# PEER layer on one core: the second product's loads asked for further ahead, and the routing replanned

## The chip, the cores and the metric

One Trainium2 chip, one core of it. The metric is the device time of one execution in microseconds (us), as the median of several runs. TensorE (PE) does matmuls; VectorE (DVE) and ScalarE (ACT) do elementwise work; GpSimd (Pool) and SyncE (SP) issue DMA transfers, each from a queue that it takes in order.

## The reference

A two-layer first block, a second block with sparse attention, and at its end the part that the change is in, a product-key expert layer (PEER) over 512 tokens of width 1024:

```python
def peer(hn, w_q, subkeys, u, v):
    H, K = PEER_HEADS, PEER_TOPK                      # 8, 16
    xt = hn.reshape(T, D)                             # 512 x 1024
    q = (xt @ w_q).reshape(T, H, 2, PEER_QDIM // 2)
    s = jnp.einsum('thcd,cnd->thcn', q, subkeys)      # 128 keys per half
    s1, i1 = lax.top_k(s[:, :, 0], K)
    s2, i2 = lax.top_k(s[:, :, 1], K)
    cand = (s1[..., :, None] + s2[..., None, :]).reshape(T, H, K * K)
    sc, ci = lax.top_k(cand, K)
    e1 = jnp.take_along_axis(i1, ci // K, axis=-1)
    e2 = jnp.take_along_axis(i2, ci % K, axis=-1)
    idx = e1 * PEER_NKEYS + e2                        # one of 16384 experts
    g = jax.nn.softmax(sc, axis=-1)
    ...
        a = jnp.einsum('cd,chkd->chk', xc, u[ic])
        act = jax.nn.gelu(a) * gc
        return jnp.einsum('chk,chkd->cd', act, v[ic])
```

All in float32.

## The kernel before

Activations are held transposed, features on partitions, tokens along the free axis. A float32 matmul is done as three with split operands (`mm3`): high weight with high and low activation, low weight with high activation. Weights come in units of 128x1024 (`wunit`): `raw` by a 512 KB load on SP's queue (three buffers), `wh` by a cast on ACT (line 279), `wl` by a subtraction on DVE (line 280). `lin2` is 24 matmuls over such a unit, at line 325.

`peer` computes 384 of the 512 tokens (SG) densely, over all 16384 experts, and the last 128 by gathers.

*Query loop* (line 1623): for each head a `lin2` with `wpq`, and the key scores go to `sco`.

*First product*: `up(e)`, e = 0 to 127 (line 1777): a `lin2` of 512 columns with unit `pu[e]`, GELU into tile `ga`; 384 of its columns are stored in DRAM as `GA[e]`, 128 in `GU[e]`. Beside it runs the routing, mostly on DVE: `route(b)` for each block of 128 tokens (the top 16 of each key half, 16 wide calls of `top16`; the candidates; the top 16 of them, 8 narrow calls; the expert numbers by compares; transposes to `e1T`, `e2T`, `gT`), and `weights(tb, share)` for 16 tokens at a time, which makes the dense gate matrix `G` in DRAM: one-hot tiles `ohA`, `ohB` (line 1736), `ohW`, a group of four matmuls for four tokens (line 1749; 96 groups in all), the two halves of the sum added into `gst` (lines 1752 and 1753), and one 1 MB write per 16 tokens on Pool's queue (line 1755, 24 of them). The routing is a generator that yields the DVE and ACT ns that a piece takes, and the loop at line 1788 puts an `up` into the program whenever the sum is above PEER_NS. Ups left when the routing is over follow in a row (line 1793). A scheduler then orders each engine's instructions; pools and their buffers set what waits for what.

*Second product*: 16 groups g of 8 experts-tiles. For each of the 8, the GELU values come back from `GA` (`gd`, 192 KB, line 1833), are multiplied in place by the group's gate block `gt` (1.5 MB of `G` in pieces of 512 B, line 1828), and split into a pair `hid` (lines 1854 and 1855; 18 buffers, so nine pairs). Then come 8 steps d, each a `lin2` of 384 columns with unit `pv[g, d]`. So there are 128 steps n = 8g + d.

*The last 128 tokens*: `rows(m)`, m = 0 to 31, gathers four tiles of 128 rows of v (`vr`, 512 KB each, eight buffers) with indirect loads on Pool; `acts(m)` gathers 4 x 128 single elements of `GU` into `ac` (four buffers) with indirect loads on Pool, then two multiplies on DVE make `az`; `sums(m)` is 16 matmuls at line 1823 that add into one accumulator. In before sums(m) stand behind step 4m + 2, and acts(m + 1) behind step 4m + 1.

## Time and profile before

| | us |
|---|---|
| median of 3 runs (3704.99 to 3709.06) | 3708.48 |
| the profiled execution | 3707.12 |
| its span | 3705.3 |
| PE busy in it | 3561.1 (96%) |
| DVE busy | 2351.8 (63%) |
| ACT busy | 1649.6 (45%) |
| Pool busy | 344.8 (9%) |
| query loop, from 2224.6 | 63.4 |
| first product with routing, 2288 to 3049 | 761 |
| no matmul, 3049 to 3071 | 22 |
| second product, 3071 to 3697 | 626 |

The stages are read off the timeline, from the first and the last instruction of a stage on PE. How to read such a profile: an engine that is busy all the time in a stage bounds it, whatever its share of the whole span; for an engine that isn't, each idle stretch has a releaser, the event that ended it, and following releasers back gives the chain of waits. A wait on the bounding engine is time lost, a wait on another engine need not be.

### The profile page before, as it was taken

What the parts mean: (1) busy time and instruction counts of PE and PEld (TensorE: products, weight loads), DVE (VectorE), ACT (ScalarE), POOL (GpSimd) and SP (SyncE); (2) the same over time, 40 slices, a digit from 0 to 9 for tenths busy, and PEclk for the clock granted to TensorE, in tenths of its full rate; (3) what the DMA queues carried; (4) which work ended last, traced back from release to release, by engine and by line L of the source; (5) the groups of instructions that cost most, each with busy time, mean ns of one, the idle gap of its engine ahead of it and who ended that gap; (6) DMA issues with size and microseconds to landing.
All of it is one profiled execution on the core that took longest, in us unless ns stands there. A gap on an engine that the chain in (4) does not pass through costs nothing.

```text
span 3705.3 us, 53755 instructions
## 1 busy us (share of the span) xinstructions
PE 3561.1 (96%) x20154; PEld 2972.7 (80%) x20154; DVE 2351.8 (63%) x4926; ACT 1649.6 (45%) x3172; POOL 344.8 (9%) x430
## 2 busy tenths in 40 slices
PE   8998999999999999998999999999999997999999
PEld 5866788888877788887878777778888876989898
DVE  5976644444688765556587568999676424555554
ACT  5267531121355742224456544568766422323332
POOL 0000000000000000000000100000000006444441
PEclk9999999999999999999999999999999998999999
DMA  6430332111242132223441242445554449888885
GB/s 213 129 114 12 117 111 74 63 63 63 86 140 90 48 129 93 95 97 121 122 131 61 75 137 84 142 161 174 188 182 167 172 152 305 302 296 295 301 301 180
DMA packets 245780, 536.03 MB, mean 145 GB/s; under 512 B 26656, under 2 KB 131424, under 8 KB 242320
## 3 DMA queue, kind: packets, MB, share of 16 engines
q1 hardware_dynamic: 215648, 426.66, 35.4%
q0 software_dynamic: 29872, 105.95, 7.6%
q8 instruction: 158, 2.59, 0.3%
q14 instruction: 102, 0.84, 0.1%
HBM read 461.09 MB, written 68.16 MB: 143 GB/s over the span
## 4 chain that ended last, share of the span: by engine, by line
PE 84%; DVE 8%; DMA 3%; ACT 3%; issue 1%; SPq 0%; POOL 0%; ACTq 0%; DVEq 0%
PE b L325 54%; PE a L325 19%; PE a L1823 2%; DVE wl L280 2%; PE b L470 1%; PE b L920 1%; DMA gd<-GA 1%; PE b L571 1%; PE a L1749 1%; PE b L909 1%; PE b L1368 1%; DMA mraw<-in_wmod_dram 1%; DVE gst L1753 1%; PE a L1128 0%; PE b L1177 0%
## 5 line engine op out<-in xcount | busy, mean ns | idle before, releaser
L279 ACT CAST wh<-raw 128x1024 fp32r<-128x1024 f32 (+2 forms) x531 | 546.9, 1031 | 1431.6 <-PE b L325 796.9
L280 DVE TENSOR_TENSOR wl<-raw,wh 128x1024 fp32r<-128x1024 f32 (+2 forms) x531 | 636.1, 1198 | 333.0 <-ACT wh L279 321.4
L325 PE MATMUL b<-hs,wh 128*128 128x512 f32 x2624 | 822.8, 395 | 4.4 <-ACT hs L1095 4.4
L325 PEld LDWEIGHTS b<-hs,wh 128*128 128x128 f32 x2624 | 489.2, 190 | 108.0 <-ACT hs L1095 5.3
L325 PE MATMUL b<-hid,wh 128*128 128x384 f32 x2048 | 534.1, 342 | 24.8 <-DMA gd<-GA 22.4
L325 PE MATMUL b<-hs,wl 128*128 128x512 f32 x1312 | 515.5, 393 | 0.0
L325 PEld LDWEIGHTS b<-hid,wh 128*128 128x128 f32 x2048 | 373.5, 189 | 53.5 <-ACT hid L1854 22.9
L325 PE MATMUL b<-hh,wh 128*128 128x256 f32 (+1 forms) x1160 | 366.1, 352 | 3.7 <-DVE V L843 2.2
L325 PE MATMUL a<-hh,wh 128*128 128x512 f32 (+1 forms) x1144 | 354.6, 348 | 9.5 <-DVE y L1049 7.2
L325 PE MATMUL b<-hl,wh 128*128 128x256 f32 (+1 forms) x1160 | 357.3, 345 | 0.3 <-DVE hl L537 0.3
L325 PE MATMUL b<-hid,wl 128*128 128x384 f32 x1024 | 348.7, 340 | 9.0 <-DVE wl L280 9.0
L325 PE MATMUL b<-hh,wl 128*128 128x256 f32 (+1 forms) x1160 | 356.0, 344 | 0.0
L325 PE MATMUL a<-hh,wl 128*128 128x512 f32 (+1 forms) x1144 | 349.6, 344 | 1.5 <-DVE wl L280 1.5
L325 PE MATMUL a<-hl,wh 128*128 128x512 f32 (+1 forms) x1144 | 350.3, 344 | 0.3 <-DVE hl L537 0.3
L325 PEld LDWEIGHTS b<-hs,wl 128*128 128x128 f32 x1312 | 248.4, 189 | 52.3 <-issue 0.2
L325 PEld LDWEIGHTS b<-hh,wh 128*128 128x128 f32 x1160 | 201.3, 189 | 44.2 <-issue 4.9
L325 PEld LDWEIGHTS a<-hh,wh 128*128 128x128 f32 x1144 | 197.0, 188 | 44.6 <-issue 13.9
L325 PEld LDWEIGHTS b<-hl,wh 128*128 128x128 f32 x1160 | 201.7, 189 | 30.4 <-issue 1.5
L325 PEld LDWEIGHTS b<-hh,wl 128*128 128x128 f32 x1160 | 201.1, 189 | 27.9 <-issue 1.1
L325 PEld LDWEIGHTS a<-hl,wh 128*128 128x128 f32 x1144 | 197.2, 188 | 31.0 <-issue 2.8
L325 PEld LDWEIGHTS a<-hh,wl 128*128 128x128 f32 x1144 | 196.9, 188 | 30.6 <-DVE wl L280 2.4
L325 PEld LDWEIGHTS b<-hid,wl 128*128 128x128 f32 x1024 | 193.8, 189 | 11.0 <-DVE wl L280 11.0
(427 smaller groups left out, 5332.6 us busy)
## 6 DMA issues: line engine op xcount, KB each, us to landing
raw<-in_w_dram SPq DMA_DIRECT2D x134, 512.0 KB
raw<-in_pu_dram SPq DMA_DIRECT2D x128, 512.0 KB
raw<-in_pv_dram SPq DMA_DIRECT2D x128, 512.0 KB
raw<-in_win_dram SPq DMA_DIRECT2D x64, 512.0 KB
mraw<-in_wmod_dram SPq DMA_DIRECT2D x82, 384.0 KB
GA<-ga SPq DMA_DIRECT2D x128, 192.0 KB
G<-gst POOLq DMA_DIRECT2D x24, 1024.0 KB, 4.7
gt<-G SPq DMA_DIRECT2D x16, 1536.0 KB
```

The source lines that it names most:

```text
L279: nc.scalar.copy(hi, raw)
L280: nc.vector.tensor_tensor(lo, raw, hi, op=OP.subtract)
L325: nc.tensor.matmul(o, w[wi], xx[xi], start=start and xi == 0 and wi == 0, stop=stop and wi == 1)
L470: nc.tensor.matmul(p[j:j + 32, 0:256], self.cs[:, k, :], ws[k], start=k < 4, stop=k >= 4, tile_position=(0, j))
L571: nc.tensor.matmul(p[:, :w], self.ones[1024], s, start=k == 0, stop=k == 7)
L909: nc.tensor.transpose(p[:, j * 128:j * 128 + 128], Ps[e][:, kc * 128:kc * 128 + 128], self.eye)
L920: nc.tensor.matmul(o[pr, c % 2 * 128:c % 2 * 128 + 128], V[i][:, kc, pr], PT[e * nkb + kc], start=kc == 0, stop=kc == nkb - 1, tile_positi ...
L1368: nc.tensor.transpose(p[:, j * 128:j * 128 + 128], src, self.eye)
L1749: nc.tensor.matmul(p[:, i * 256:i * 256 + 256], A[:, i], W[:, i].rearrange("p j e -> p (j e)"), start=True, stop=True)
L1753: nc.vector.tensor_tensor(gst[:, :, t8:t8 + 4].rearrange("p e t -> p t e"), q[:, :, 0], lo, op=OP.add)
L1823: nc.tensor.matmul(po[32 * j:32 * j + 32, h:h + 512], z[:, j, :], v[j][:, h:h + 512], start=m == 0, stop=m == 31, tile_position=(0, 32 * j))
```

## The change

The routing and its plan. The sum of DVE time and that of ACT time are each compared with a limit of their own, and the yields have other numbers. `route(0)` is begun inside the query loop, two of its wide top-16 calls after each head but the first. The low half of a gate product is copied to `glo` with tokens innermost, and the add into `gst` reads its operands in that order and writes runs of four.

The border. Tile `ga` has moved to the early pool `rg`, which stays open, so that the same six buffers serve the loads back from `GA`. `ups` left over when the routing is done are now put into the program after the second product's pool is open: two gate blocks and two sets of rows are asked for ahead of them, four `ga` loads ahead of the last two of them, two behind them, then the elements of four sums.

The second product. A gate block is loaded in four quarters (six token blocks each, 384 KB in 768 pieces), on Pool's queue, two groups ahead, at steps d = 0, 2, 4, 6. A `ga` load is asked for right behind the multiply that frees its buffer; the product goes to a tile of its own, `pr`. The elements of sums m + 4 are asked for behind sums(m), and the gate times the one-hot, `zg`, is made by a Pool multiply; a single DVE multiply by the elements, `gated(m)`, stands before the step in front of the sums. Sums stand at steps 2 + 120m//31 (every 3.87 steps, the last at 122; before 126). (Its yields in `route` went from 1000, 600, 7000 and 1800 to 1770, 1270, 12500 and 2400, not shown.)

```diff
-PEER_NS = 3620
-ROUTE_NS = 800
+PEER_NS = (4230, 3800)
+ROUTE_NS = 1320
...
-        ru = fr.enter_context(self.tc.tile_pool(name="ru", bufs=1))
-        for h in range(8):
-            p = self.lin2(a["wpq"][h], hs)
-            q = self.g2("q")
...
+
+        r0 = route(0)
+        for h in range(8):
+            p = self.lin2(a["wpq"][h], hs)
...
+            if h:
+                next(r0)
+                next(r0)
...
-                yield (2300, 0) if dve else (1200, 2350)
+                yield (2750, 0) if dve else (1380, 3170)
...
                 q = p.rearrange("p (t j e) -> p t j e", t=4, j=2)
-                lo = self.t("glo", [128, 4, 128], bufs=1, pool=rt)
-                nc.scalar.copy(lo, q[:, :, 1])
-                nc.vector.tensor_tensor(gst[:, :, t8:t8 + 4].rearrange("p e t -> p t e"), q[:, :, 0], lo, op=OP.add)
-                yield 600, 550
+                lo = self.t("glo", [128, 128, 4], bufs=1, pool=rt)
+                nc.scalar.copy(lo, q[:, :, 1].rearrange("p t e -> p e t"))
+                nc.vector.tensor_tensor(gst[:, :, t8:t8 + 4], q[:, :, 0].rearrange("p t e -> p e t"), lo, op=OP.add)
+                yield 700, 580
...
-            for ns in route(0):
+            for ns in r0:
                 yield ns, 0
...
         def up(e):
             p = self.lin2(a["pu"][e], hs)
-            ga = self.t("ga", [128, S], bufs=NGA, pool=ru)
+            ga = self.t("ga", [128, S], bufs=NGA, pool=rg)
             nc.scalar.activation(ga, p, AF.Gelu_apprx_tanh)
             GA[e] = dp.tile([128, SG], F32, name=f"GA{e}")
...
         for ns in routing():
             due = [x + y for x, y in zip(due, ns)]
-            while max(due) > PEER_NS and todo:
-                due = [max(x - PEER_NS, 0.0) for x in due]
+            while todo and any(x > y for x, y in zip(due, PEER_NS)):
+                due = [max(x - y, 0.0) for x, y in zip(due, PEER_NS)]
                 up(todo.pop(0))
-        for e in todo:
-            up(e)
         fr.close()
         rb = self.es.enter_context(self.tc.tile_pool(name="rb", bufs=1))
-        VR, gas, gts = {}, {}, {}
+        VR, AC, AZ, gas, gts = {}, {}, {}, {}, {}
 
...
         def acts(m):
 
-            c = self.t("ac", [128, 4], bufs=4, pool=rb)
+            c = AC[m] = self.t("ac", [128, 4], bufs=4, pool=rb)
+            z = AZ[m] = self.t("zg", [128, 4, 32], bufs=4, pool=rb)
+            nc.gpsimd.tensor_tensor(z, G3[:, m::32][:, :, None].to_broadcast([128, 4, 32]), hot[:, None, 31 - m:63 - m].to_broadcast([128, 4, 32]), op=OP.mult)
             for j in range(4):
                 t = 32 * j + m
                 nc.gpsimd.indirect_dma_start(out=c[:, j:j + 1], out_offset=None, in_=GU.rearrange("e p (t o) -> (e p t) o", o=1),
                                              in_offset=bass.IndirectOffsetOnAxis(ap=IG[:, t:t + 1], axis=0))
-            nc.vector.tensor_tensor(c, c, G3[:, m::32], op=OP.mult)
-            z = VR[m] = self.t("az", [128, 4, 32], bufs=3, pool=rb)
-            nc.vector.tensor_tensor(z, c[:, :, None].to_broadcast([128, 4, 32]), hot[:, None, 31 - m:63 - m].to_broadcast([128, 4, 32]), op=OP.mult)
+
+        def gated(m):
+
+            z = self.t("az", [128, 4, 32], bufs=1, pool=rb)
+            nc.vector.tensor_tensor(z, AZ[m], AC.pop(m)[:, :, None].to_broadcast([128, 4, 32]), op=OP.mult)
+            AZ[m] = z
 
         def sums(m):
-            z = VR.pop(m)
+            z = AZ.pop(m)
             v = [VR.pop((m, j)) for j in range(4)]
             for h in range(0, D, 512):
                 for j in range(4):
                     nc.tensor.matmul(po[32 * j:32 * j + 32, h:h + 512], z[:, j, :], v[j][:, h:h + 512],
                                      start=m == 0, stop=m == 31, tile_position=(0, 32 * j))
 
-        def load_gt(g):
-            gts[g] = self.t("gt", [128, NTB, 8, TBW], bufs=2, pool=rb)
-            nc.sync.dma_start(out=gts[g].rearrange("p b e t -> p b (e t)"),
-                              in_=G[:, :, 8 * g:8 * g + 8, :].rearrange("b p e t -> p b (e t)"))
+        def load_gt(g, q=range(4)):
+            if 0 in q:
+                gts[g] = self.t("gt", [128, NTB, 8, TBW], bufs=2, pool=rb)
+            for i in q:
+                bs = slice(i * NTB // 4, (i + 1) * NTB // 4)
+                nc.gpsimd.dma_start(out=gts[g][:, bs].rearrange("p b e t -> p b (e t)"),
+                                    in_=G[bs, :, 8 * g:8 * g + 8, :].rearrange("b p e t -> p b (e t)"))
 
         def load_ga(e):
-            gas[e] = self.t("gd", [128, SG], bufs=8, pool=rb)
+            gas[e] = self.t("ga", [128, S], bufs=NGA, pool=rg)[:, :SG]
             nc.sync.dma_start(out=gas[e], in_=GA[e])
 
         hot = rb.tile([128, 64], F32, name="hot")
         nc.gpsimd.memset(hot, 0.0)
         nc.gpsimd.memset(hot[:, 31:32], 1.0)
         load_gt(0)
-        for e in range(8):
-            load_ga(e)
+        load_gt(1)
         for m in range(2):
             rows(m)
+        for e in todo[:-2]:
+            up(e)
+        for e in range(NGA - 2):
+            load_ga(e)
+        for e in todo[-2:]:
+            up(e)
+        for e in range(NGA - 2, NGA):
+            load_ga(e)
+        for m in range(4):
+            acts(m)
         po = self.acc()
-        acts(0)
+        at = {2 + 120 * m // 31: m for m in range(32)}
         for g in range(16):
             gt = gts.pop(g)
             hid = []
             for e in range(8):
-                ga = gas.pop(8 * g + e)
-                gv = ga.rearrange("p (b t) -> p b t", t=TBW)
-                nc.vector.tensor_tensor(gv, gv, gt[:, :, e, :], op=OP.mult)
+                gv = gas.pop(8 * g + e).rearrange("p (b t) -> p b t", t=TBW)
+                ga = self.t("pr", [128, SG], bufs=2, pool=rb)
+                nc.vector.tensor_tensor(ga.rearrange("p (b t) -> p b t", t=TBW), gv, gt[:, :, e, :], op=OP.mult)
+                if 8 * g + e + NGA < 128:
+                    load_ga(8 * g + e + NGA)
                 hi = self.t("hid", [128, SG], F32R, 18, rb)
                 lo = self.t("hid", [128, SG], F32R, 18, rb)
                 nc.scalar.copy(hi, ga)
                 nc.vector.tensor_tensor(lo, ga, hi, op=OP.subtract)
                 hid.append((hi, lo))
-            if g < 15:
-                load_gt(g + 1)
             for d in range(8):
-                if g < 15:
-                    load_ga(8 * g + 8 + d)
+                if g < 14 and d % 2 == 0:
+                    load_gt(g + 2, [d // 2])
+                n = 8 * g + d
+                if n + 1 in at:
+                    gated(at[n + 1])
                 p = self.lin2(a["pv"][g, d], hid, n=SG)
                 nc.vector.tensor_tensor(X[d][:, :SG], X[d][:, :SG], p, op=OP.add)
-                m, r = divmod(8 * g + d, 4)
-                if r == 1 and m < 31:
-                    acts(m + 1)
-                if r == 2:
+                if n in at:
+                    m = at[n]
                     sums(m)
                     if m < 30:
                         rows(m + 2)
+                    if m < 28:
+                        acts(m + 4)
         y = self.t("vr", [128, D], bufs=NVR, pool=rb)
         nc.scalar.copy(y, po)
         for h in range(2):
```

How it moves instructions, in three places. First DVE, at the first one-hots of the first product; before (`mr`, `sc`, `ci` are tiles of the narrow top-16 of the next block, `wl` an up's weights):

```order
L1649 MAX sc_22101<-cand_22049 128x8
L1652 MAX sc_22101<-mr_22213 128x8
L1650 MAX_INDEX ci_22102<-sc_22101,cand_22049 128x8
L1653 MAX_INDEX ci_22102<-sc_22101,mr_22213 128x8
L1651 MATCH_REPLACE mr_22255<-sc_22101,cand_22049 128x50
L1649 MAX sc_22101<-cand_22049 128x8
L280 TENSOR_TENSOR wl_21507<-raw_21504,wh_21506 128x1024
L1736 TENSOR_TENSOR ohA_21364<-iota,e1T 128x512
L1736 TENSOR_TENSOR ohB_21365<-iota,e2T 128x512
```

and now:

```order
L1656 TENSOR_TENSOR cand_22126<-tv_21374 128x8x8
L1639 MAX_INDEX ti_21375<-tv_21374,mr_22076 128x8
L1656 TENSOR_TENSOR cand_22126<-tv_21374 128x8x16
L1656 TENSOR_TENSOR cand_22126<-tv_21374 128x8x5
L1656 TENSOR_TENSOR cand_22126<-tv_21374 128x8x4
L280 TENSOR_TENSOR wl_21454<-raw_21451,wh_21453 128x1024
L1740 TENSOR_TENSOR ohA_21325<-iota,e1T 128x512
L1740 TENSOR_TENSOR ohB_21326<-iota,e2T 128x512
L1711 TENSOR_TENSOR glT<-gT,ghT 128x128
L1740 TENSOR_TENSOR ohA_21432<-iota,e1T 128x512
L1740 TENSOR_TENSOR ohB_21433<-iota,e2T 128x512
```

The first one-hots came behind a run of narrow top-16 rows; now the last row of the routing ahead of them is the sum of candidates, and the wide top-16s of the next block stand further forward.

Second, Pool's queue where the second product begins (`g_20229` is the gate tile of the last block, `hot` a row with a single one); before:

```order
L1755 DMA G<-gst_27349 128x2048
L1836 MEMSET hot 128x64
L1804 DMA vr_28463<-in_vn_dram,iv 128x1024
L1837 MEMSET hot 128x1
...
L1804 DMA vr_28477<-in_vn_dram,iv 128x1024
L1812 DMA ac_28480<-GU,ig 128x1 x4
L1812 DMA ac_28598<-GU,ig 128x1 x4
...
L1812 DMA ac_29322<-GU,ig 128x1 x3
L1804 DMA vr_28648<-in_vn_dram,iv 128x1024
...
L1812 DMA ac_29322<-GU,ig 128x1
```

and now:

```order
L1759 DMA G<-gst_27922 128x2048
L1846 MEMSET hot 128x64
L1838 DMA gt_28153<-G 128x6x128
L1847 MEMSET hot 128x1
L1838 DMA gt_28153<-G 128x6x128 x3
L1838 DMA gt_28158<-G 128x6x128 x4
L1806 DMA vr_28163<-in_vn_dram,iv 128x1024
...
L1806 DMA vr_28177<-in_vn_dram,iv 128x1024
...
L1813 TENSOR_TENSOR zg_28480<-g_20229,hot 128x128
...
L1816 DMA ac_28479<-GU,ig 128x1 x4
...
L1838 DMA gt_28572<-G 128x6x128 x2
L1806 DMA vr_28681<-in_vn_dram,iv 128x1024
```

The eight `vr` loads stand behind eight quarter loads of gate blocks now, and the quarter loads of later groups stand between `vr` and `ac`. On PE nine `ups` follow the last weights group, where 25 did.

Third, SP's queue at a border between two groups; before:

```order
L1833 DMA gd_30264<-GA_23869 128x384
L285 DMA raw_30174<-in_pv_dram 128x1024
L1833 DMA gd_30340<-GA_23938 128x384
L285 DMA raw_30216<-in_pv_dram 128x1024
L1828 DMA gt_30700<-G 128x24x128
L285 DMA raw_30266<-in_pv_dram 128x1024
L285 DMA raw_30342<-in_pv_dram 128x1024
L285 DMA raw_30376<-in_pv_dram 128x1024
L285 DMA raw_30418<-in_pv_dram 128x1024
L285 DMA raw_30468<-in_pv_dram 128x1024
L285 DMA raw_30502<-in_pv_dram 128x1024
L1833 DMA gd_30374<-GA_24009 128x384
```

and now:

```order
L1843 DMA ga_31145<-GA_24785 128x384
L285 DMA raw_31069<-in_pv_dram 128x1024
L1843 DMA ga_31153<-GA_24821 128x384
L285 DMA raw_31103<-in_pv_dram 128x1024
L285 DMA raw_31201<-in_pv_dram 128x1024
L285 DMA raw_31256<-in_pv_dram 128x1024
L285 DMA raw_31289<-in_pv_dram 128x1024
L285 DMA raw_31323<-in_pv_dram 128x1024
L285 DMA raw_31356<-in_pv_dram 128x1024
L1843 DMA ga_31161<-GA_24857 128x384
```

The gate block is gone from SP's queue, six units of `pv` still stand in a row, and the `ga` loads in front of them are those that the next group's first multiplies release.

## Rows read from the trace of the kernel before

**Rows 1.** Windows by stage: us, busy us (instructions) by engine, PEclk, DMA share, GB/s.

```profile
2224.60:2288.00 63.40, 63.22 (x300) 50.36 (x301) 46.98 (x185) 30.26 (x60) 0.54 (x1) 0.95 0.21 66
2288.00:2500.00 212.00, 201.48 (x910) 165.83 (x909) 211.28 (x846) 128.84 (x301) 2.67 (x5) 0.98 0.45 148
2500.00:3049.00 549.00, 548.85 (x2550) 456.61 (x2548) 339.58 (x598) 332.47 (x771) 10.09 (x19) 1.00 0.50 172
...
3071.00:3136.00 65.00, 57.76 (x314) 50.61 (x315) 37.41 (x75) 19.69 (x28) 39.78 (x40) 0.93 0.90 279
3136.00:3697.00 561.00, 556.52 (x3277) 506.30 (x3276) 306.48 (x498) 174.74 (x226) 229.81 (x204) 1.00 0.81 281
```

**Rows 2.** The chain of waits, first product: start us, us, what.

```profile
2529.47 5.48 PE b L325 x24
2535.43 5.48 PE b L325 x24
...
2912.81 135.83 PE b L325 x599
```

**Rows 3.** Timeline of PE, first product: start, us, instruction, [idle before <-releaser].

```profile
2356.75 1.46 PE L1749 MATMUL a<-ohW,ohA 128*128 128x256 f32 x4 [5.43 <-ACT ohW L1745]
...
2458.63 1.45 PE L1749 MATMUL a<-ohW,ohA 128*128 128x256 f32 x4 [3.77 <-ACT ohW L1745]
```

**Rows 4.** DVE, first product: two timeline rows, then a group (mean ns, idle).

```profile
2346.76 0.43 DVE L1670 TENSOR_TENSOR cand<-tv 128x24 f32<-128x24 f32 x3
...
2353.75 0.69 DVE L1736 TENSOR_TENSOR ohA<-iota,e1T 128x512 fp32r<-128x512 f32 x1
...
L1753 DVE TENSOR_TENSOR gst<-a,glo 128x512 f32<-128x512 f32 x96 | 100.9, 1051 | 5.9 <-ACT glo L1752 5.9
```

**Rows 5.** The gap between the products: chain (first row), timeline of SP, of PE.

```profile
3050.60 1.70 DMA GU<-ga
...
3052.56 0.38 SPq L1828 DMA_DIRECT2D gt<-G  x1
3053.00 15.34 SPq L1833 DMA_DIRECT2D gd<-GA  x8
...
3071.29 0.69 PE L325 MATMUL b<-hid,wh 128*128 128x384 f32 x1 [22.43 <-DMA gd<-GA]
```

**Rows 6.** The chain of waits, second product.

```profile
3087.74 1.85 PE a L1823 x16
...
3133.86 1.85 PE a L1823 x16
3135.71 17.10 PE b L325 x96
3152.81 1.85 PE a L1823 x16
...
3304.38 1.85 PE a L1823 x16
...
3327.21 1.85 PE a L1823 x16
```

**Rows 7.** Second product: chain, timeline of DVE, of SP.

```profile
3101.75 7.87 DMA ac<-GU,ig
...
3109.65 0.17 DVE L1814 TENSOR_TENSOR ac<-ac,g 128x4 f32<-128x4 f32 x1 [9.79 <-DMA ac<-GU,ig]
...
3289.98 19.94 SPq L285 DMA_DIRECT2D raw<-in_pv_dram  x6
```

**Rows 8.** Pool's groups (mean ns; idle), and one issue (median us to landing).

```profile
L1804 POOL DMA_INDIRECT vr<-in_vn_dram,iv x128 | 154.3, 1205 | 284.6 <-PE a L1823 244.0 <-issue 27.6 <-PE b L325 13.0
L1812 POOL DMA_INDIRECT ac<-GU,ig x128 | 127.8, 999 | 41.9 <-issue 34.3 <-DMA vr<-in_vn_dram,iv 3.9 <-DVE x L1863 2.4
L1755 POOL DMA_DIRECT2D G<-gst x24 | 12.8, 532 | 669.0 <-DVE gst L1753 515.2 <-DVE gz L1681 46.5 <-DVE ci L1653 34.8
...
ac<-GU,ig POOLq DMA_INDIRECT x128, 6.5
```

29 lines of the change are left out of this document (15 added, 14 removed).

## The prediction

> **What bounds the kernel now.** I read the stretches first, by stage. From the first product to the last of the second, TensorE is nearly always busy: 548.85 of 549 us in the second part of the first product, 556.52 of 561 in the long part of the second [rows 1]. So nothing can be won there by a faster VectorE or a faster load; only the places where PE stands still, or where it was given a lower clock, are to be had. They are four: the first 212 us of the first product (PE 201.48 busy, clock .98, DVE 211.28 of 212: VectorE is the bound in this stretch and in no other) [rows 1], the gap between the two products [rows 5], the 65 us behind it (clock .93) [rows 1], and three borders between groups later on [rows 6]. All of them lie in stretches that the change rewrites, and there is nothing else in the diff that touches the time before 2224 us.
>
> **What TensorE's own work would take.** In the first product 599 matmuls ran in 135.83 us without a wait [rows 2]: .2268 us each, 24 of them 5.443 us an up. Where a weights group stands between two ups the ups begin 2535.43 - 2529.47 = 5.96 us apart [rows 2], so a group adds .512. 128 ups and 96 groups are 128 x 5.443 + 96 x .512 = 696.7 + 49.2 = 746 us. The stage took 3049 - 2288 = 761 [rows 1], so 15 us of it are waits and clock. Two waits carry 5.43 + 3.77 = 9.2 of it [rows 3], both for the one-hots of a weights group; the clock of .98 over 212 us is another 4.
>
> In the second product sums and four steps alternate, 1.85 + 17.09 us, 18.95 from one sums to the next [rows 6]; 27 of the 31 periods are so, and a step is 17.09/4 = 4.273. What is above that is loss.
>
> **The up stage: -13.** The wait of 5.43 comes from the order on DVE: behind the wl of an up stands a run of narrow top-16 rows of the next block's routing, from 2346.76 on, and the first one-hot starts at 2353.75 [rows 4]. In the changed order the wl is followed directly by ohA and ohB, so this wait goes. What is late next is DVE itself. Adding the row durations up by up, DVE's work in before runs ahead of PE's 5.6 us an up by some 29 us at its worst (about the 45th up); in the new order by some 16 us (about the 34th), then falls below zero. Three things do that: 14 of the 16 wide top-16s of the first block move into the query loop, the routing is spread over 16 more ups (25 ups in a row stand behind the last weights group in before, 9 in after), and the write of the gate block has another form. The first of them costs: 14 x about 1.2 us of DVE is 17 us, and the query loop has 63.40 - 46.98 = 16.4 us of DVE to spare [rows 1]. That just fits, and where it doesn't the ups behind it wait; I take 2 us for this and for what is left of the 16 us excess (0 to 6). The new write form is not in the trace: the add of before takes 1051 ns with a strided write, an operation of equal size with contiguous write .69 [rows 4]; the new one writes runs of four and reads PSUM in a stride, so .69 to 1.05. I take 1.05, since it stays strided on one side; at .69 DVE gains 35 us over the stage, all of it where DVE isn't the bound but for the first third. So of 15 us lost I give back 13 and 2 are the new residue of the move into the query loop, which leaves the sum at -13 + 2 = -11.
>
> **The gap: -22.4.** PE stood 22.43 us between the last up and the first step [rows 5]. All loads of the second product are asked for only when the first is over (gt at 3052.56 and eight gd from 3053.00 on [rows 5]). In after, the pool of the second product opens with nine ups still to run; Pool asks for both first gate blocks and eight vr there, SP for four ga before the last two ups. 9 x 5.443 = 49 us cover 1.5 + 1.5 + 4 MB: 7 MB in 49 us is 143 GB/s on top of the stage's 172 [rows 1], about what the second product moves at full rate (281 [rows 1]), hence tight but enough; the vr can land later. Without that cover the 22.4 us would be back.
>
> **Behind the gap: -11.8.** The first sums began at 3087.74, 16.4 us after 3071.29 instead of 3 x 4.273 = 12.8: 3.6 us. The third sums began at 3133.86, 46.1 us later, where two periods are 37.9: 8.2 too many [rows 6]. Two causes show. DVE stood 9.79 us on the ac elements with the wl of a step queued behind it, the one that PE then waited for; the elements were issued at 3101.75 and took 7.87 us to land [rows 7], since Pool's queue holds them in one row with the vr. In after the elements of the first four sums are asked for ahead of the first step, later ones four sums ahead, and DVE's multiply stands one step before its sums. The other is the gd again, of the next group.
>
> One new cost is here. The first four acts need the last up's store to GU. That store was out at 3050.60 + 1.70 = 3052.3 in before, and the last up ended 22.43 us ahead of 3071.29, at 3048.9 [rows 5]: 3.4 us. Four issues of .95 and .3 between them, then 6.5 us to land [rows 8]: 3.4 + 3 x 1.25 + 6.5 = 13.7 us behind the end of the ups, and the first sums want them at 12.8, with a small DVE multiply in between. I take 2 us; 0 if they land like the store, in 1.70, and 3 with the 7.87 of the late ac.
>
> **Borders: -7.0.** The largest is 3304.38 to 3327.21, 22.83 instead of 18.95: 3.9 us [rows 6]. Two more of the same look cost 2.1 and 1.0. In each PE waited for a wl that stood on DVE behind a multiply which waited for gd; and the gd were late since SP, which takes its queue in order, stood 19.94 us on six raw loads [rows 7] ahead of them. In after the ga loads hang on the multiply that frees their buffer, and the order shows those for e = 6, 7 of the next group behind this group's border, 34 us ahead of use. gt is gone from SP and asked two groups ahead.
>
> **What the change adds on Pool.** 64 quarter loads and 32 multiplies. In before Pool issued 24 plain writes, .53 us each [rows 8]; a quarter load has 768 pieces of 512 B where an ac has 128 elements. Between two sums (3.87 steps, 3.87 x 4.273 + 1.85 = 18.4 us) Pool has 4 vr at 1.205 and 4 ac at 1.0, each with .3 between [rows 8], plus about .3 for the small multiply: 11.5 us. 6.9 us are left for 1.94 quarters. Break-even is a quarter of 6.9/1.94 - .3 = 3.25 us. The nearest row is the plain write at .53, a plain copy as a quarter is; I take .5 to 1 and charge nothing. The farthest bound is one piece by one: 6 x .947 = 5.7 us, the slower rival. Below nothing is excluded: SP loses only 16 issues of .37.
>
> I put 2 us on the rest of the second product (ga buffers are six instead of eight; `pr` has two), bounds 0 and 18: at worst 1.2 us at each of 15 borders.
>
> **Sum**, on the profiled execution's span: 3705.3 - 13 + 2 (up stage) - 22.4 - 11.8 - 7.0 (gap, start, borders) + 2 (first acts) + 2 (rest) = 3657. That execution took 3707.12, 1.8 more than its span, and the median is 1.4 above it: 3660.
>
> **Rivals.**
>
> A: *the waits move to the front of the second product.* The loads come earlier, but the first ac come late, the ga of six buffers come late at borders, or 7 MB ahead of the border press the last ups' raw loads. For it: the DMA engines are at .90 and at .81 busy [rows 1], and nine ups' loads run beside. Against: the steady periods ran at 281 GB/s [rows 1], raw loads among them, with no loss. 3 (acts) + 1.2 x 15 (borders) less the 4 already counted = 17 us: 3677.
>
> B, *slower: Pool's queue becomes the bound.* vr, ac and gt quarters are on one in-order queue; if a quarter takes 5.7 us to issue, Pool needs 11.5 + 1.94 x 6.0 = 23.1 us for 18.4, and each sums comes 4.7 us late, over 28 of them 133, less a period that the lookahead absorbs: +114, so 3774. It makes the kernel slower than before by over .2% from (56 + 18.4)/28 = 2.7 us a period, 4.6 us a quarter, on. For it: a vr took from .93 to 2.0 us in this stage, with a mean of 1.205 [rows 8], so Pool's issues lengthen beside other work. Against: 2.1 times is the largest seen, and on .53 that is 1.1. The Trainium skill, SBUF — State Buffer, section "A bandwidth-pool intuition that's wrong (but worth ruling out)", tells of a GpSimd DMA of about 620 ns alone that takes about 3100 ns beside a VectorE copy; by that a quarter would be an estimated five times .53, 2.7 us, still under 3.25, but with little left. The same skill's page DMA: Bandwidth & Descriptors, section "Issuing engine by pattern", gives simple loads to Sync and speaks against this move; no row here has a plain load on Pool.
>
> C: *the change doesn't do what it says.* The second product's waits are not late requests but bandwidth: 281 GB/s at .81 is what the queues give, and 512 B pieces are dear. Then the borders and 8 us of the start stay: 15 us, 3675. Against: the 27 steady periods, at the same rate, are all 18.95.
>
> **How the numbers follow.** Forecast .70 (its own range 3648 to 3670: residues of 6 us gone and 3 us from the clock of .95 in the query loop [rows 1] below, 10 of the bounds above), A .14, B .09, C .07. The predicted time is the forecast's. The range goes to 3692 to hold A and C with their spread, and a light B; the low end is 3646. What a measurement of this kernel can tell from no change is about .2%, 7.4 us. Slower by that: .08 (B beyond 4.6 us); within: .03; faster: .89.
>
> **What would show it.** Up stage: PE's wait of 5 us before the first weights groups gone, the stage 748 to 752 us from first to last up. Gap: PE idle under 2 us, gt loads landing under the ups. Second product: sums 18.4 us apart from the first on, DVE never waiting for ac beyond the first; SP free of gt. Pool: a quarter under 1.1 us, its idle before vr named by PE's sums. Wrong would be: a Pool without idle time, PE waiting for vr or az; or DVE on gt at a border; or a late first one-hot still behind top-16 rows.

## The result, and the profile after

The changed kernel takes 3663.01 us (median of 4 runs, 3659.8 to 3668.04) beside 3708.77 for the kernel before in the same comparison: ratio .9879, 95% interval .9862 to .9896, a gain of 45.8 us. The forecast was 3660. The profiled execution has a span of 3660.9 us.

The windows by stage, after (us, busy us and instructions by engine in the order PE, PEld, DVE, ACT, Pool, then PEclk, DMA share, GB/s; as [rows 1], with the stretch ahead of the change first):

```profile
0.00:2215.62 2215.62, 2124.47 (x12806) 1735.51 (x12807) 1404.64 (x2717) 962.38 (x1787) 49.19 (x147) 0.99 0.31 100
2215.62:2279.00 63.38, 63.20 (x302) 50.40 (x303) 47.00 (x185) 30.50 (x61) 0.54 (x1) 0.96 0.21 68
2279.00:2491.00 212.00, 208.17 (x944) 172.49 (x944) 211.40 (x909) 127.43 (x290) 2.67 (x5) 0.98 0.46 148
2491.00:3030.80 539.80, 539.80 (x2513) 449.22 (x2512) 315.60 (x542) 334.45 (x784) 27.23 (x41) 1.00 0.55 189
3030.80:3084.00 53.20, 48.70 (x277) 42.23 (x279) 28.73 (x46) 16.92 (x24) 38.52 (x37) 1.00 0.73 240
3084.00:3652.00 568.00, 567.73 (x3312) 508.23 (x3313) 324.51 (x489) 174.58 (x229) 303.97 (x295) 1.00 0.82 286
```

the last nine ups of it by themselves:

```profile
2982.00:3030.80 48.80, 48.80 (x216) 40.35 (x215) 15.02 (x17) 14.91 (x22) 17.64 (x23) 1.00 0.90 323
```

and in the kernel before that first stretch, up to the query loop, and the first 5.6 us of the second product:

```profile
0.00:2224.56 2224.56, 2132.75 (x12807) 1742.64 (x12807) 1406.42 (x2717) 962.10 (x1787) 49.09 (x147) 0.98 0.31 99
...
3071.29:3076.89 5.60, 4.53 (x12) 3.41 (x13) 4.63 (x10) 2.24 (x5) 3.51 (x4) 0.50 1.11 319
```

The reader should see two things. The window in which DVE was the bound still has DVE busy 211.4 of 212, but PE now 208.17 where [rows 1] has 201.48. And the execution enters the query loop at 2215.62 where the one before came there at 2224.56: 8.9 us of the difference between the two profiled spans lie ahead of everything that the change touches. PE ran the same 12,806 or 12,807 matmuls there, busy 8.3 us longer in the one profile than in the other, at a granted clock of .98 against .99. The change writes nothing there. Over the fourteen profiles below this entry lies between 2213.4 and 2224.6 us (2217.7 to 2224.6 in the three kernels built on the one before, 2213.4 to 2222.0 in the eleven built on the changed one); why the clock differs from execution to execution no run shows.

What is left from the query loop to the last step of the second product is 1472.1 us before and 1436.6 after: 35.5. The waits of PE in it (timeline, start, us, instruction, idle before and releaser), which answer to [rows 3, 5]:

```profile
2340.33 1.46 PE L1753 MATMUL a<-ohW,ohA 128*128 128x256 f32 x4 [3.83 <-ACT ohW L1749]
...
3038.31 0.62 PE L325 MATMUL b<-hid,wh 128*128 128x384 f32 x2 [1.20 <-ACT hid L1875]
...
3046.11 1.92 PE L1830 MATMUL a<-vr,az 128*32 128x512 f32 x16 [0.89 <-issue]
3049.11 0.45 PE L325 MATMUL b<-hid,wl 128*128 128x384 f32 x1 [0.53 <-DVE wl L280]
```

The .89 us ahead of the first sums have "issue" as their releaser; DVE's row beside it shows what was late, the elements:

```profile
3045.76 0.29 DVE L1822 TENSOR_TENSOR az<-zg,ac 128x128 f32<-128x128 f32 x1 [4.74 <-DMA ac<-GU,ig]
```

The 22.43 us between the products are gone: the last up ends and the first step begins at 3030.80. One of the two long waits for one-hots is left, 3.83 us. Pool's quarter loads, and the add into gst (mean ns; idle), which answer to [rows 8, 4]:

```profile
L1838 POOL DMA_DIRECT2D gt<-G x64 | 55.4, 878 | 22.6 <-DVE pr L1870 21.0 <-DMA vr<-in_vn_dram,iv 1.2 <-issue 0.3
...
L1757 DVE TENSOR_TENSOR gst<-a,glo 128x512 f32<-128x512 f32 x96 | 65.4, 682 | 3.5 <-ACT glo L1756 3.5
```

A quarter load takes .878 us to issue; the add into gst .682 where it was 1.051.

One thing did not move. DVE ran 185 instructions in the query loop before [rows 1] and 185 after, 47 us in both. The wide top-16s that the change begins there in the program were there already in the kernel before, put there by the scheduler (rows of its tile `sco` from 2224.6 to 2288: count, ns at least, in the middle and at most, first and last start):

```profile
L1651 DVE MATCH_REPLACE8 mr<-tv,sco x14: 273/275/280, 2242.2 to 2282.9; 128x128 f32<-128x128 f32 x14
```

### The profile page after: what moved, and what is told of

Same layout as the page of the kernel before. It is cut to its first block, busy times and chain, and to the rows that moved or that the text cites. A ratio compares the mean times of both kernels' runs of the same rounds, so it can differ in the third digit from the quotient of the medians.

```text
span 3660.9 us, 53707 instructions
## 1 busy us (share of the span) xinstructions
PE 3553.2 (97%) x20154; PEld 2958.9 (81%) x20154; DVE 2334.0 (64%) x4894; ACT 1646.3 (45%) x3172; POOL 422.1 (12%) x526
## 3 DMA queue, kind: packets, MB, share of 16 engines
q1 hardware_dynamic: 166240, 401.50, 33.3%
q0 software_dynamic: 37040, 131.12, 10.0%
## 4 chain that ended last, share of the span: by engine, by line
PE 87%; DVE 6%; ACT 3%; DMA 2%; issue 1%; SPq 0%; DVEq 0%; ACTq 0%
PE b L325 57%; PE a L325 19%; PE a L1830 2%; PE b L470 1%; PE b L920 1%; PE a L1753 1%; DVE wl L280 1%; PE b L571 1%; PE b L909 1%; PE b L1368 1%; PE a L1128 0%; ACT P L899 0%; DMA mraw<-in_wmod_dram 0%; PE b L1177 0%; DMA mg<-in_wmod_dram 0%
## 5 line engine op out<-in xcount | busy, mean ns | idle before, releaser
L1885 DVE TENSOR_TENSOR x<-x,b 128x384 f32<-128x384 f32 x128 | 70.5, 551 | 206.4 <-PE b L325 172.3
```

Of the source, the lines that this page charges most:

```text
L1885: nc.vector.tensor_tensor(X[d][:, :SG], X[d][:, :SG], p, op=OP.add)
```

## The experiments

All readings of a stage are taken from PE's timeline of the profiled execution: the entry into the query loop, the ups (from the last query-key matmul to the end of the last up), the gap between the products, the second product (from its first matmul to the end of the last step) and the sum from the entry on. In the ideal, 128 steps of 4.273 and 32 sums of 1.85 make a second product of 606.1 us. Medians move by some us from the clock in the first 2200 us (the entries show it), so the stages tell more than the medians. Each stage is read from a single execution, though. Kernels with the changed kernel's first product have ups from 750.7 to 752.2, and old_gst, whose second product is the changed kernel's, has 617.7 there beside 621.4: a difference of 1.5 us in the ups, or of 4 us in the second product, shows nothing by itself.

| kernel | median us | ratio to before, 95% | entry | ups | gap | second product | from entry |
|---|---|---|---|---|---|---|---|
| before | 3708.77 | | 2224.6 | 760.8 | 22.4 | 625.3 | 1472.1 |
| changed | 3663.01 | .9862 to .9896 | 2215.6 | 752.2 | 0 | 621.4 | 1436.6 |
| whole_sums | 3662.32 | .9865 to .9901 | 2213.4 | 750.8 | 0 | 620.9 | 1435.2 |
| ups_first | 3676.76 | .9902 to .9946 | 2214.1 | 750.8 | 3.2 | 635.2 | 1452.2 |
| gt_sync | 3690.63 | .9916 to .9956 | 2222.0 | 759.9 | 0 | 639.5 | 1462.2 |
| old_plan | 3666.39 | .9870 to .9906 | 2216.7 | 756.0 | 0 | 620.5 | 1439.0 |
| old_gst | 3664.81 | .9869 to .9901 | 2216.5 | 755.3 | 0 | 617.7 | 1436.6 |
| acts2 | 3661.27 | .9861 to .9893 | 2215.3 | 750.9 | 0 | 619.6 | 1434.0 |
| inplace | 3695.42 | .9959 to .9985 | 2214.9 | 750.7 | 0 | 653.4 | 1467.1 |
| inplace_hid20 | 3658.02 | .9850 to .9883 | 2216.8 | 752.2 | 0 | 614.8 | 1430.1 |
| best_a | 3654.64 | .9843 to .9876 | 2219.3 | 752.2 | 0 | 610.8 | 1425.9 |
| best_b | 3656.83 | .9847 to .9881 | 2218.4 | 752.1 | 0 | 611.6 | 1426.7 |
| before_gtpool | 3721.53 | 1.0026 to 1.0052 | 2217.7 | 760.7 | 18.7 | 651.8 | 1494.5 |
| before_newgst | 3700.65 | .9970 to .9996 | 2219.3 | 755.2 | 20.2 | 635.3 | 1474.2 |

**Sums kept whole**

```diff
-        at = {2 + 120 * m // 31: m for m in range(32)}
+        at = {2 + 4 * m: m for m in range(32)}
```

> Sums stand behind steps 4m + 2, as in the kernel before; all else as in the changed kernel. In the changed kernel four sums (behind steps 32, 40, 48 and 56, each the first step of a group) stand on PE in three pieces of 1, 4 and 3 rows between matmuls of the step, and the pieces took .97, .99 and .99 us where a whole one takes 1.85. Theory (the split costs): no sums in pieces, each of the four borders 1.1 to 1.5 us shorter, 4.4 to 6 us in all; with four steps between the first and the second sums instead of three, most of the 3.8 us that are lost there go too: 5 to 9 us off, 3654 to 3658 where the changed kernel has 3663. Rival (the border's 1.5 us are hid pairs that come late, and the scheduler only filled that time with sums): the four borders keep their 1.5 us as waits of PE for hid, and the time stays within 2 us of the changed kernel's.

In the changed kernel four sums stand in pieces. The chain of waits at the first of them (start, us, what):

```profile
3193.09 0.98 PE a L1830 x2
3194.07 0.55 PE b L325 x2
3194.62 1.00 PE a L1830 x8
3195.61 0.38 PE b L325
3195.99 0.99 PE a L1830 x6
```

Three pieces of PE's work at line 1830, .98 + 1.00 + .99 us, where a sums in one piece takes 1.85: 1.1 us more. From the sums before to the sums behind such a border the changed kernel takes 1.5 to 1.8 us more than steps and sums would. In whole_sums there are no pieces, and the chain reads:

```profile
3105.38 1.85 PE a L1830 x16
3124.81 1.85 PE a L1830 x16
3143.77 1.85 PE a L1830 x16
```

From 3105.38 to 3124.81 are 19.43 us, to 3143.77 18.96: every second period, the one with a border in it, costs some .45 (.2 to .64 over all). So both were half right: the pieces cost what was said, but without them the fifteen borders cost 6.5 us in all where the changed kernel's borders cost 8.5; that it is hid pairs that come late is tried below. The start did not gain from the longer way to the second sums: it lost 1.3 us more than in the changed kernel, with PE's half pace again (see acts2). The second product gains .6 us, which is within the spread.

**Ups ahead of the pool**

```diff
+        for e in todo:
+            up(e)
         fr.close()
...
-        for e in todo[:-2]:
-            up(e)
         for e in range(NGA - 2):
             load_ga(e)
-        for e in todo[-2:]:
-            up(e)
         for e in range(NGA - 2, NGA):
```

> The ups that are left when the routing is done run before the second product's pool is opened, as in the kernel before; all else as in the changed kernel. Theory (the nine ups are the cover of the first loads): PE's wait between the products is back, 18 to 23 us (22.43 in the kernel before), and the time is 3681 to 3687. Rival (asking gate blocks from Pool's queue and keeping the ga buffers in the early pool is what removed the gap): a gap of 5 us or less, 3663 to 3668.

```profile
3031.14 0.44 PE L325 MATMUL b<-hid,wh 128*128 128x384 f32 x1 [3.18 <-ACT hid L1873]
...
3042.97 0.69 PE L325 MATMUL b<-hid,wh 128*128 128x384 f32 x1 [3.92 <-DVE hid L1874]
...
3086.65 1.50 PE L325 MATMUL b<-hid,wh 128*128 128x384 f32 x2 [5.50 <-ACT hid L1873]
```

These are PE's three longest waits. The gap is 3.18 us and not 22: the theory falls. The rival has the gap right and the time wrong (3676.76 where it had 3663 to 3668). What the kernel before waited for is in its timeline of Pool, at the first instruction of the new pool:

```profile
3052.87 0.16 POOL L1836 MEMSET hot<- 128x64 f32 x1 [136.62 <-DMA GU<-ga]
```

By that releaser `hot` got memory that the ups' `ga` tiles had held, so Pool, with everything behind it, stood until the last up's store to GU was over. In the changed kernel `ga` lies in the early pool, and the same memset waits 5.05 us for the last write of G only; in ups_first it waits 5.15, at 2987.19, so where the ups are written does not matter for it (changed kernel):

```profile
2990.09 0.16 POOL L1846 MEMSET hot<- 128x64 f32 x1 [5.05 <-DMA G<-gst]
...
2991.44 5.75 POOL L1838 DMA_DIRECT2D gt<-G  x7
```

The place of the ups still matters, for SP's queue: with all `ga` loads behind the last up, nine of them stand in a row on SP ahead of the next raw, and hid pairs come late in the first two groups. From the entry on the kernel takes 15.6 us more than the changed one: the three waits above are 12.6, and behind them the clock is .84 over the first 65 us of the second product, where the changed kernel has 1.00. No run has `ga` in the early pool and nothing else of the change; that the memory held the queue is read from the releaser, and that the place of the ups did not is shown here.

**Gate blocks from SP's queue**

```diff
-                nc.gpsimd.dma_start(out=gts[g][:, bs]...
+                nc.sync.dma_start(out=gts[g][:, bs]...
```

> The quarter loads of the gate blocks are asked for from SP's queue, as in the kernel before, at the same places of the program; all else as in the changed kernel. Theory (what counts is how far ahead they are asked for, not whose queue): PE's borders as in the changed kernel, within 3 us, 3660 to 3667; Pool has 64 issues of .88 us less and its vr and ac come no later. Rival (SP's queue in order is what made the border waits): raw and ga loads stand behind quarters again, PE waits for wl or hid at several borders, 5 to 10 us more, 3668 to 3673.

```profile
2996.24 20.01 SPq L1838 DMA_DIRECT2D gt<-G  x8
```

(timeline of SP, then of ACT and PE)

```profile
3023.46 1.04 ACT L279 CAST wh<-raw 128x1024 fp32r<-128x1024 f32 x1 [12.96 <-DMA raw<-in_pu_dram]
...
3024.55 0.74 PE L325 MATMUL b<-hs,wh 128*128 128x512 f32 x2 [3.81 <-ACT wh L279]
```

Eight quarter loads held SP's queue for 20.01 us, where Pool had issued seven in 5.75; the units of the last ups stood behind them, ACT waited 12.96 us for raw and PE 3.81 for the cast. The ups lose 7.7 us, what the rival said, though at the ups and not at the borders: 3.81 are this wait, and right behind it the clock was granted at half, 1.2 GHz, for 6.82 us (some 3.15 us lost, half of the 6.30 that PE was busy in it, an estimate):

```profile
3025.17:3031.99 6.82, 6.30 (x16) 4.82 (x16) 3.04 (x3) 2.72 (x4) 0.00 (x0) 0.50 0.86 259
```

The borders are as in the changed kernel, so loads two groups ahead do keep them on either queue. The other 18 us, in the second product, are of another kind (timeline of PE, then the window):

```profile
3080.46 0.48 PE L325 MATMUL b<-hid,wh 128*128 128x384 f32 x1 [1.71 <-issue]
```

```profile
3066.00:3089.00 23.00, 8.28 (x20) 4.95 (x19) 1.44 (x2) 0.00 (x0) 15.26 (x18) 0.58 0.49 157
```

From 3066 to 3089 PE did 20 matmuls, 1.15 us apart on average where .178 is the rule (4.273 / 24), and the trace names no releaser; that is 19 us, and neither theory had it (more of this below, at acts2). The clock was .58 in this window, but it fell to half only at 3069.54, when the slow pace had begun. The runs of this kernel went from 3668 to 3695, so it may not be there in every execution. The DMA queues of both kernels (packets, MB, share of 16 engines), first the changed one:

```profile
q1 hardware_dynamic: 166240, 401.50, 33.3%
q0 software_dynamic: 37040, 131.12, 10.0%
```

```profile
q1 hardware_dynamic: 216416, 426.67, 35.3%
q0 software_dynamic: 29872, 105.95, 7.8%
```

The 25.17 MB of gate blocks are 216416 - 166240 = 50,176 packets on SP's queue, 502 B each on average, but 37040 - 29872 = 7,168 on Pool's, 3.5 KB each.

**The same queue in the kernel before**

```diff
-            nc.sync.dma_start(out=gts[g].rearrange(...
+            nc.gpsimd.dma_start(out=gts[g].rearrange(...
```

> The kernel before, with its sixteen loads of a whole gate block (3072 pieces of 512 B) asked for from Pool's queue instead of SP's, at the same places of the program; nothing else. In the kernel before, eight gd issues took 15.34 us on SP behind such a load, and in the run gt_sync eight quarters took 20.01 us on SP where seven took 5.75 on Pool. Theory (such loads hold up SP's queue, and on Pool they don't): the eight gd issues take 3 to 4 us, PE's wait between the products is 12 to 17 us instead of 22.4, the three borders' 7 us go; 3690 to 3700. Rival (the time ahead is what counts, not the queue): the gap within 3 us of 22.4, the borders late as they are, 3705 to 3712, or more where Pool's vr and ac now wait behind the blocks.

```profile
3045.35 3.71 SPq L1833 DMA_DIRECT2D gd<-GA  x8
...
3059.20 1.03 DVE L1851 TENSOR_TENSOR gd<-gd,gt 128x384 f32<-128x384 f32 x2 [15.44 <-DMA gt<-G]
...
3154.07 0.69 PE L325 MATMUL b<-hid,wh 128*128 128x384 f32 x1 [7.43 <-DVE hid L1855]
```

Those are rows of SP, of DVE and of PE. The theory's first sign is there: the eight gd issues take 3.71 us, where 15.34 passed from the first to the last in the kernel before [rows 5]. But the gap is 18.7, neither the theory's 12 to 17 nor quite the rival's 19.4 or more: DVE's first multiply now waited 15.44 us for the gate block itself, since Pool could ask for it only at 3046.14, behind the memset that waits for the last store. The second product grows to 651.8, with PE waits of 1.8 to 7.4 us at nine of the fifteen borders, as at 3154.07. DVE waited 97.3 us for ac in this stage, in fifteen waits, and Pool for DVE to free a gate buffer (who, for what: us in all, times, longest):

```profile
POOL gt L1828 <- DVE gd L1851: 92.4, 11, 9.9
```

A block asked for one group ahead stands on Pool's queue until DVE has freed its buffer, and the ac and vr behind it stand with it. The kernel is slower than before, as the rival's second case had it. So the queue alone is a loss. gt_sync, which has the whole change but the queue, is .4 to .8% faster than the kernel before; of what it lacks against the changed kernel 7.7 us are the queue's, and the slow pace of the other 18 is open.

**The old plan**

```diff
-PEER_NS = (4230, 3800)
+PEER_NS = (3620, 3620)
...
-            if h:
-                next(r0)
-                next(r0)
```

and the old yields and ROUTE_NS.

> The planner's numbers are those of the kernel before (limit 3620, the old yields), and the first block's routing isn't begun in the query loop; the new form of the gate write and the rest as in the changed kernel. Theory (the plan takes the excess off DVE): from the first up to the last 758 to 762 us instead of 752.0, with 5 us waits of PE at the first weights groups; 25 ups stand behind the last group, and the time is 3669 to 3673. Rival (the add into gst, 682 ns now where it was 1051, has taken the excess off by itself): 752 to 754 us, 3663 to 3665.

```profile
2347.96 1.46 PE L1750 MATMUL a<-ohW,ohA 128*128 128x256 f32 x4 [5.38 <-ACT ohW L1746]
...
2447.05 1.26 PE L1750 MATMUL a<-ohW,ohA 128*128 128x256 f32 x4 [0.97 <-ACT ohW L1746]
```

The ups take 756.0, between the two expectations: the 5.4 us wait of [rows 3] is back, the second is down to .97. The plan is worth 3.8 us of the 8.6 when the new form is there, and it is the limits and yields that bring it: DVE's 185 instructions in the query loop are there in old_plan too.

**The old and the new form of the gate write**

```diff
-                lo = self.t("glo", [128, 128, 4], bufs=1, pool=rt)
-                nc.scalar.copy(lo, q[:, :, 1].rearrange("p t e -> p e t"))
+                lo = self.t("glo", [128, 4, 128], bufs=1, pool=rt)
+                nc.scalar.copy(lo, q[:, :, 1])
```

with the add to match; and the reverse of it in the kernel before.

> The gate product is copied and added in the form of the kernel before (a strided write of 1051 ns on DVE where the new form takes 682); all else as in the changed kernel. Theory (after the new plan DVE isn't the bound): 96 x .37 = 35 us more DVE work, but only what falls into the first third counts; from the first up to the last 752 to 756 us where the changed kernel has 752, the total 3663 to 3668. Rival (the new form is what relieved DVE, the plan little): 758 us or more, the waits for one-hots back, 3669 or more.

> The kernel before with the new form of the gate write alone (glo with tokens innermost, the add writing runs of four). The add took 682 ns in the changed kernel where it took 1051. Theory (DVE is the bound of the first 212 us of the first product): its rows of weights groups lie in that stretch too, DVE ahead of PE by some 10 us less, the waits for one-hots 5.4 + 3.8 + .8 shrink to about 6 to 7, from the first up to the last 756 to 759 us where the kernel before has 760.8; the total 3704 to 3708. Rival (the waits come from the order of DVE's rows, which this doesn't move): 760 to 761, 3707 to 3710.

PE's waits for one-hots in the first product (us in all, times, longest), in the kernel before and in before_newgst:

```profile
PE a L1749 <- ACT ohW L1745: 10.3, 4, 5.4
```

```profile
PE a L1749 <- ACT ohW L1745: 6.9, 3, 5.4
```

With the old form in the changed kernel the ups take 755.3, 3.1 more; with the new form in the kernel before they take 755.2, 5.6 less. The first theory holds, and the second a little beyond its range. So either alone, plan or form, brings 5 to 6 us of the 8.6, and the other adds 3 to 4. The second product of before_newgst, 635.3 beside 625.3, has more waits for wl at borders; its edit doesn't touch that stage, and no second profile shows whether other executions have them. Its median is lower than that of the kernel before, by .04 to .30%.

**Elements two sums ahead**

```diff
-        for m in range(4):
+        for m in range(2):
             acts(m)
...
-                    if m < 28:
-                        acts(m + 4)
+                    if m < 30:
+                        acts(m + 2)
```

> The elements are asked for two sums ahead instead of four (8 gathers ahead of the first step instead of 16); all else as in the changed kernel. In the changed kernel PE ran from 3055.0 to 3059.7 at half its pace, with gaps for which the trace names nothing, while Pool issued 16 gathers of ac without a pause; the second sums then came 3.8 us late. Theory (the run of gathers delays PE's instructions): no such gaps, the second sums 1 to 4 us earlier, second product 617.5 to 620.5 us where the changed kernel has 621.4. Rival (the gaps have another cause, and two ahead is too late): the gaps stay, or DVE waits for ac at sums further on, second product 621 to 630 us.

In the changed kernel PE ran at half its pace for a while, with gaps that name no releaser, during a run of sixteen gathers (timeline of PE, the window, then Pool):

```profile
3058.21 0.60 PE L325 MATMUL b<-hid,wh 128*128 128x384 f32 x2 [0.57 <-issue]
```

```profile
3055.00:3060.00 5.00, 3.12 (x14) 2.36 (x14) 0.21 (x1) 0.24 (x1) 4.23 (x5) 1.00 0.31 84
```

```profile
3036.47 0.98 POOL L1816 DMA_INDIRECT ac<-GU,ig  x1 [24.52 <-DMA GU<-ga]
...
3057.13 0.94 POOL L1816 DMA_INDIRECT ac<-GU,ig  x1 [0.30 <-DMA ac<-GU,ig]
```

That is 14 matmuls in 5 us, where 28 would fit, at a clock of 1.00. It looks like what gt_sync showed for longer. In acts2 these gaps are gone and the second sums come 2.2 us earlier, counted from the first step; the second product is 1.8 us shorter, no wait for ac came further on. That fits the theory; but the runs old_gst, inplace and inplace_hid20 have the sixteen gathers and no such gaps, so the run of gathers is at most a part of the cause, and 1.8 us is within the spread of the second product. What holds PE back there stays open.

**The multiply in place, and more hid buffers**

```diff
-                ga = self.t("pr", [128, SG], bufs=2, pool=rb)
-                nc.vector.tensor_tensor(ga.rearrange("p (b t) -> p b t", t=TBW), gv, gt[:, :, e, :], op=OP.mult)
-                if 8 * g + e + NGA < 128:
-                    load_ga(8 * g + e + NGA)
-                hi = self.t("hid", [128, SG], F32R, 18, rb)
+                nc.vector.tensor_tensor(gv, gv, gt[:, :, e, :], op=OP.mult)
+                hi = self.t("hid", [128, SG], F32R, 20, rb)
...
                 nc.vector.tensor_tensor(lo, ga, hi, op=OP.subtract)
+                if 8 * g + e + NGA < 128:
+                    load_ga(8 * g + e + NGA)
```

(20 in the second run, 18 in the first; in both the sums stand at 4m + 2, as in whole_sums)

> Sums behind steps 4m + 2 as in the run whole_sums, and the gate multiply in place in the ga buffer, as in the kernel before, with the load that takes the buffer next behind the split; no tile pr. In whole_sums each border between groups cost .43 to .49 us, 15 times, with multiply, cast and subtraction taking turns (two buffers of pr). Theory (pr's two buffers hold the multiplies back): the borders cost under .1, the second product 613 to 616 us where whole_sums has 620.9, total 3655 to 3659. Rival (the borders wait for hid buffers, or for DVE's sum of work there): .4 us a border stay, 619 to 622.

> As the run inplace, and 20 hid buffers instead of 18, so that two pairs of the next group can be made ahead. Theory (pr's two buffers were the limit): as inplace within 1 us. Rival (the hid buffers are the limit): the borders' .4 us go here and not in the run inplace, 613 to 616 against 619 to 622.

The first, at its first border (timeline of DVE, of PE):

```profile
3073.41 0.56 DVE L1870 TENSOR_TENSOR ga<-ga,gt 128x384 f32<-128x384 f32 x1 [4.23 <-DMA ga<-GA]
...
3074.57 0.45 PE L325 MATMUL b<-hid,wh 128*128 128x384 f32 x1 [2.30 <-ACT hid L1873]
```

With 18 hid buffers the load of a ga can only be asked for when the border's own splits are done, and arrives in the middle of that border: 1.4 to 5.5 us at each, 45 in all; the second product is 32 us longer than the changed kernel's. Neither theory nor rival had that. It shows what `pr` is for: the load hangs on the multiply, which doesn't need a hid buffer. With two pairs more, the splits run ahead, and nearly every period is clean:

```profile
3129.10 1.85 PE a L1830 x16
3148.05 1.85 PE a L1830 x16
```

```profile
3082.23 0.56 DVE L1870 TENSOR_TENSOR ga<-ga,gt 128x384 f32<-128x384 f32 x1 [10.10 <-DMA gt<-G]
```

The first two are of the chain, the last is of DVE: 18.95 us at border and elsewhere. What is left is one wait of DVE at the second border, 10.10 us for a quarter of the third gate block, since multiplies now run ahead of the loads. The second product of 614.8 is what the rival had for 20 buffers. So the number of hid pairs makes the borders' cost; no run has `pr` and 20 buffers, so a part of `pr`'s two buffers in the .45 us is not excluded.

**The good parts together**

> The run inplace_hid20 with the elements asked for two sums ahead as in the run acts2: the parts that the earlier runs found good, together. Theory (the two gains are at different places and add): the second product 612 to 615 us where inplace_hid20 has 614.8 and the changed kernel 621.4; median 3653 to 3658. Rival (they have the start of the second product in common, and DVE there still waits for a gate block's quarter as in inplace_hid20): 614 to 616, median 3657 to 3660.

> As the run best_a, with the first sums one step later (behind step 3). In the changed kernel PE waited .9 us for the first az, whose elements landed 15 us behind the last up. Theory (the first elements are late by about 1 us): this wait goes, 1 to 1.5 us less than best_a. Rival (what waits next, the first wl or the second gate block, is late just the same): within .5 us of best_a.

best_a is inplace_hid20 with acts2; best_b has the first sums one step later. The second product takes 610.8 us, 4.7 above the ideal, less than theory and rival gave; from the entry on it is 10.7 us shorter than the changed kernel. DVE's 10.10 us for the third gate block are not among its waits any more; that eight gathers fewer ahead of that block on Pool's queue are the reason is likely, not shown. Its median is 3654.64, ratio to before .9859 (.9843 to .9876), and it is the fastest kernel here; the interval overlaps that of the changed kernel, whose own comparison was another. best_b differs from it by nothing that counts, as its rival had it (timeline of DVE):

```profile
3046.82 0.29 DVE L1822 TENSOR_TENSOR az<-zg,ac 128x128 f32<-128x128 f32 x1 [3.31 <-DMA ac<-GU,ig]
```

DVE still stood 3.31 us on the elements, with the next wl behind it, and PE waited 1.81 us for that wl (at 3050.17) instead of az: the wait moved and did not go.

## Why the prediction was right in time and wrong in its parts

- **Ups, -11 forecast: -8.6.** The mechanism holds (old_plan, old_gst, before_newgst). Of the two 5.43 and 3.77 waits one of 3.83 is left: in the new order ohA and ohB do follow the wl, but wl comes at 2336.19, behind the wide top-16s that now stand there. That step said "so this wait goes"; it only shrank, and a late first one-hot behind top-16 rows was among the forecast's own signs of being wrong. The first of the three things named for DVE's excess, the 14 wide top-16s that move into the query loop, was no change at all: the kernel before had them there, and [rows 1]'s 46.98 us hold them. Of the 13 us given back some 4 were the clock of .98 in the first 212 us; it is .98 in that window after the change too, so that part did not come. The add into gst was sized at its upper bound; it measured .682, the lower one.
- **Gap, -22.4 forecast: -22.4.** Right in size, wrong in what lets the loads start. The forecast named the nine ups behind the pool's opening in the program; in ups_first they stand ahead of it, and Pool asks for the gate blocks under them all the same, since with `ga` in the early pool it isn't held by the last store. "Without that cover the 22.4 us would be back" is refuted for the place in the program: 3.18 us came back. That the loads fit under the ups was right. 143 + 172 GB/s are 315, more than the 281 that the forecast set beside it, but in the 48.8 us of the last nine ups the DMA moved 323, and PE was busy in all of them.
- **Start, -11.8 + 2 forecast: -5.0.** From the first step to the third sums the changed kernel loses 2.5, 3.8 and .5 us where the kernel before lost 11.8. The forecast gave the whole 11.8 back by the elements and the gd. But of the 3.6 us that the kernel before lost ahead of its first sums some 2.3 were the clock, at half behind the gap (half of the 4.53 us that PE was busy from 3071.29 to 3076.89, an estimate). The first elements term had the lateness right (15 us from the last up to landing where 13.7 was worked out) and charged 2 us where PE waited .89 for the first az; another 1.20 was a hid pair whose `ga` was late. Most of the 3.8 us were not in the sum: PE's half pace.
- **Borders and rest, -7.0 + 2 forecast: +1.1.** From the third sums on the kernel before lost 7.4 us, the changed kernel 8.5. The failed step is the one that charged 2 us for the rest with a bound of 1.2 a border: the waits for gd did go, but four sums in pieces cost 6.4 and other borders another 2. That the four sums stand in pieces could be read in the order of PE's instructions beforehand; the prediction took the places of the sums, and not whether their rows stay together.
- **Pool, 0 forecast.** The quarter at .878 us lies in the range of .5 to 1 that was taken, far from 3.25. The estimate of 2.7, worked out from the Trainium skill's page SBUF — State Buffer, section "A bandwidth-pool intuition that's wrong (but worth ruling out)", did not come, with DVE busy 324.5 of 568 us beside the quarters; the page speaks of a VectorE copy, and DVE's groups in this stage are all operations on two tensors, so the page's own case is not tried here. The Trainium skill's page DMA: Bandwidth & Descriptors, section "Issuing engine by pattern", gives simple loads to Sync; gt_sync measures the opposite for loads in 512 B pieces, 7.7 us in the ups, and before_gtpool agrees with the page where a block is asked for only one group ahead. "SP loses only 16 issues of .37" was the wrong price: in gt_sync eight quarters hold SP's queue for 20.01 us.
- **The sum.** In its own stretch the change gave 35.5 us where 48.2 were forecast, 12.7 too many. That the total came out 3 us from the forecast is luck: it is owed to the 8.9 us by which the two profiled executions differ ahead of the change, and to medians that move by as much. How far the change's own part of the 45.8 us goes beyond 35.5 stays open: the profiled execution of the kernel before has the latest entry of all fourteen here (2213.4 to 2224.6), and each kernel's stages are known from one execution. Nor does a run separate what `zg` on Pool, the earlier elements and the earlier gate blocks each brought at the start.
- **Rivals.** A came true in part, and for the second product it was nearer than the forecast: that stage is 15.3 us above the ideal where the forecast's terms leave 4 and A's 21. Waits did move to the start and the borders, but 6 to 7 us are the pieces and some 3 PE's half pace, which A did not name, and the raw loads of the last ups were not pressed. B was far off. C fell: the waits for gd are gone with the DMA at 286 GB/s where the kernel before had 281.

## What to carry to other kernels

When loads of the next stage all start late, look at the memory they land in before their place in the program: one tile of the old stage in that memory holds the whole queue. A large load in small pieces belongs on a queue where nothing urgent stands behind it, and far ahead; here the queue alone was a loss, and the rest of the change without the queue lost 7.7 us in the ups. And when an order of instructions is to be judged, see whether runs of matmuls that go together stay whole.

## What the hardware showed that I had not expected

- The same load of 512 B pieces: 20.01 us of SP's queue for eight quarters, some 6.6 of Pool's, and 50,176 packets against 7,168.
- Sixteen matmuls on four column groups take 1.85 us in one run; 2, 8 and 6 of them between others take .98, 1.00 and .99: a piece costs about the same whatever it holds.
- PE went at half pace for some 5 us in three kernels (the changed one, whole_sums, old_plan) at the same place, with no releaser (in the changed kernel at a granted clock of 1.00), and at a sixth of its pace for 23 us in gt_sync (20 matmuls, clock .58). Open.
- Behind a wait of PE the clock was granted at half: 6.82 us behind the 3.81 us of gt_sync, 5.60 us and more behind the 22.43 us between the products. So these waits cost more than their own length.
